# A hybrid decoder layer on one core: the first softmax heads of a set start one group later, and the gated GLA rows are turned one step later

## Chip, core and metric

The kernel runs on one core of a Trainium2 chip, in one launch. The metric is the device time of that launch in microseconds, the median of several executions. TensorE (PE in the profile) multiplies, VectorE (DVE) and ScalarE (ACT) do the elementwise work, GpSimd (POOL) does a few small steps, and SyncE (SP) issues nearly all DMAs, in order.

## The reference, cut to what matters

One layer, 512 tokens, width 2048, float32. After a first RMSNorm one projection feeds two groups of heads: four heads of gated linear attention (GLA), whose rows are normalised and multiplied by silu of a gate, and eight softmax heads. Both results go through `w_out`, and a SwiGLU block of hidden width 5632 follows.

```python
h = rms_norm(x, norm1_g[l])
proj = h @ w_in[l]
qa, ka, va, ra, ga, qb, kb, vb = jnp.split(proj, split_points, axis=-1)
...
out_a = gla_mixer(qa, ka, va, ra, log_g, gla_onorm_g[l])   # ... * silu(ra)
out_b = dilated_mixer(rms_norm(qb), rms_norm(kb), vb, rel_bias)
mix = jnp.concatenate([out_a, out_b], axis=-1)
x = x + mix @ w_out[l]
h2 = rms_norm(x, norm2_g[l])
x = x + (silu(h2 @ w_gate[l]) * (h2 @ w_up[l])) @ w_down[l]
```

(Reshapes are left out here.) For the softmax heads the three dilated branches, merged by their denominators, come to one causal softmax over 512 keys with a bias table per distance.

## The kernel before

**The stream of products.** All large matrix products are done as pairs of 512 columns (`Pair`, L199). A pair's product over 512 rows and 1024 columns is computed by a Strassen-like scheme of seven products P1 to P7 on operand blocks A11, A12, A22 and sums S1 to S4. Each product takes four *groups* of 256 contraction rows, so a pair has 28 groups. `stream` (L301) runs all pairs in one loop over groups. For each group a weight tile of 128x1024 is needed as it is or as a difference of two tiles (`source`, L219; the subtraction is L230 on VectorE); ScalarE casts its high part (`wh`, L320), VectorE makes the low part (`wl`, L324), and TensorE runs eight products with `wh` and then four with `wl` (L364). The buffers for `wh` and `wl` are two each, so the casts run about one group ahead of TensorE. In this document groups are counted in TensorE's order from 1: the first pair is 1 to 28, the four projection pairs after it 29 to 140, the pair of the GLA gate columns 141 to 168 ("gate pair"), and the first pair of `w_out` begins at 169.

**The work between the products.** In the middle of each group, between the `wh` and the `wl` products, the pair's `step` is called (L371). It first counts down what was put off with `later` (L503 to L512) and then takes units from the generators in `background`, in the order of the list, until it has spent as many units as the pair's pace allows (L515 to L523). `soon` (L377) puts something off by whole groups. `ensure` (L328) hurries the background when the next group's operand is not made yet. The order in which the instructions land on an engine follows from this emission and from the scheduler of the framework, and it is fixed when the program is built; each engine and the SP queue then run in that order.

**The softmax heads.** `dil_heads(h)` (L1052) runs two heads in two lanes. Stage 0 of `dil_head` (L962) issues the loads of q, k (L981), v (L985) and the bias table (L987); stage 1 scales q on ScalarE (L991); the stages after it compute scores (L999), add bias and take the maximum on VectorE (L1004), exponentiate on ScalarE (L1008), scale on VectorE (L1014, L1015), turn the result on TensorE (L1026, copied back at L1029) and multiply with the values (L1033, copied at L1036). The last stage stores the head to `mix_d` (L1049). Heads 0 to 3 are set 0 and run in the groups from 113 on; heads 4 to 7 are set 1 and run in the gate pair. After stage 0 of the first heads of a set (h = 0 and h = 4) the generator yields once more than the others (L1062).

**What reads the heads.** `early_jobs` (L1249) loads finished heads back (`top`, L1226), splits them as A11 (L178 on ScalarE, L179 on VectorE), and subtracts their halves (`differ`, L1264 on VectorE) for S3. `late_jobs` (L1285) makes S1, S2, S4, A12 and A22 from heads and gated rows (L1295, L1297, L1299). All are operands of the `w_out` pairs.

**The gated rows.** The gate pair ends in `final_gate` (L1191), once for each of four blocks (half, which): first (0,0), then (1,1), (0,1), and (1,0) out of the accumulators after the last product. It multiplies the normalised GLA rows with the gate column (L1207, or L1200), builds the sigmoid on ScalarE with three activations (L1208 or L1205, L1209, L1210), and two groups later `rest` multiplies both (L1214) and puts `transposed_store` (L1158) off with `later`. That does eight transposes on TensorE (L1165), two copies on ScalarE (L1173) and two stores to `mix_d` (L1180).

Of the kernel before, what the change touches and what calls it, by code (L numbers as in the profile page):

```python
# [108 lines left out]
def block_kernel(ctx: ExitStack, tc: tile.TileContext, ins, out):  # L109
# [19 lines left out]
    def nm(s):  # L129
        uid[0] += 1  # L130
        return f"{s}_{uid[0]}"
# [4 lines left out]
    def bank():  # L136
        return ps.tile([P, 512], F32, name=nm("bank"), tag="bank")

    def work(tag, shape=(P, 512), bufs=1):
        return mp.tile(list(shape), F32, name=nm(tag), tag=tag, bufs=bufs)  # L140
# [51 lines left out]
    def unfolded(t):  # L192

        return t.rearrange("p (a b) -> p b a", b=2)

    def halves(t):
        return t.rearrange("p (b a) -> p b a", b=2)
# [179 lines left out]
    def soon(fn, groups=1):  # L377

        soonest.append([groups, fn])
# [123 lines left out]
    def later(units, fn, hold=False):  # L503

        deferred.append([units, fn, hold])
# [546 lines left out]
    def dil_heads(h):  # L1052

        lanes = [dil_head(h, 0), dil_head(h + 1, 1)]
        for i in range(8):
            for n, lane in enumerate(lanes):
                for rest in next(lane) or ():
                    rest()
                if i == 7 and n == 1:
                    done.update((id(mix_d[4 + h // 2]), half) for half in range(2))  # L1060
                yield 0.5
            if i == 0 and h % 4 == 0:  # L1062
                yield

    def together(*gens):

        gens = list(gens)
        while gens:
            spent = WAIT
            for g in list(gens):  # L1070
                try:
                    cost = next(g)
                except StopIteration:
                    gens.remove(g)
                    cost = 0.0
                cost = 1.0 if cost is None else cost
                if cost >= 0:
                    spent = max(spent, 0.0) + cost
            yield spent
# [23 lines left out]
    def heads_norm(t, then):  # L1103
# [8 lines left out]
        def rest():  # L1112
# [11 lines left out]
        "va0": lambda: [gla_head(0), gla_head(1)],  # L1124
        "va1": lambda: [gla_head(2), gla_head(3)],
        "vb0": lambda: [dil_heads(0), dil_heads(2)],
        "qb1": lambda: [
            together(dil_heads(4), put_off(8, early_jobs(opm, (0, 1), mix_d[4:], True))),
            together(dil_heads(6), put_off(2, early_jobs(opm, (2,), mix_d[4:], True)), late_opm[0]),
            early_jobs(opm, (3,), mix_d[4:], True),  # L1130
            late_opm[1],
# [26 lines left out]
    def transposed_store(tiles, half, dsts, gains=None, spare=None):  # L1158

        for b in range(2):  # L1160
            bk = bank().rearrange("p (j n) -> p j n", j=2)
            for jj in range(2):
                for m in range(2):
                    f = (2 * b + jj) * P
                    nc.tensor.transpose(  # L1165
                        bk[:, jj, m * P : (m + 1) * P], tiles[m][:, f : f + P], ident
                    )
            if spare is None:
                d = work(("oT", "PT")[b], (P, 2, 256))
            else:  # L1170
                d = spare[:, b]
            if gains is None:
                nc.scalar.copy(d, bk)  # L1173
            else:
                for jj in range(2):
                    nc.scalar.activation(
                        d[:, jj, :], bk[:, jj, :], AF.Copy,
                        scale=gains[:, 2 * b + jj : 2 * b + jj + 1],
                    )
            store(dsts[b][:, :, half * 256 : (half + 1) * 256], d)  # L1180
            done.add((id(dsts[b]), half))
# [9 lines left out]
    def final_gate(half, which, tiles, acc_):  # L1191
        og = onorm.pop((half, which))
        if tiles is None:
            tiles = [cpool.tile([P, 512], F32, name=nm("cr"), tag="C") for _ in range(2)]
            src = acc_
        else:
            src = tiles
        for m in range(2):
            if src is acc_:
                nc.vector.scalar_tensor_tensor(  # L1200
                    halves(og[m]), unfolded(src[m]), row_scale(half, m), halves(og[m]),
                    op0=ALU.mult, op1=ALU.mult,
                )
                neg = nrs1[:, 2 * half + m : 2 * half + m + 1]
                nc.scalar.activation(halves(tiles[m]), unfolded(src[m]), AF.Exp, scale=neg)  # L1205
            else:
                nc.vector.tensor_tensor(og[m], src[m], og[m], op=ALU.mult)  # L1207
                nc.scalar.activation(tiles[m], src[m], AF.Exp, scale=-1.0)  # L1208
            nc.scalar.activation(tiles[m], tiles[m], AF.Ln, bias=1.0)  # L1209
            nc.scalar.activation(tiles[m], tiles[m], AF.Exp, scale=-1.0)  # L1210

        def rest():
            for m in range(2):
                nc.vector.tensor_tensor(tiles[m], tiles[m], og[m], op=ALU.mult)  # L1214
            spare = apool.tile([P, 2, 2, 256], F32, name=nm("turned"), tag="A")
            later(1 + (src is tiles), lambda: transposed_store(
                tiles, half, mix_d[2 * which : 2 * which + 2], spare=spare
            ))

        soon(rest, 2)  # L1220
# [561 lines left out]
```

## Time and profile before

| what | value |
|---|---|
| median of three runs | 1939.63 us (1934.64 to 1940.75) |
| the profiled execution's own time | 1940.65 us |
| its span, first to last instruction | 1938.9 us |
| mean granted TensorE clock | 0.997 |
| DMA, mean over the span | 187 GB/s |

The profile shows one execution. A timeline row reads: start, duration, engine, line, operation, output and inputs, how many, and in square brackets the idle time before it and what ended it. A row of the waits reads: who waited at which line for whom; total us, times, longest us. In rows of stretches each engine has its busy time and its number of instructions, and after them stand the granted clock of TensorE, the DMA share and GB/s. Idle time of an engine that is not the bottleneck costs nothing.

### The profile page before, as it was taken

What the parts mean: (1) busy time and instruction counts of PE and PEld (TensorE: products, weight loads), DVE (VectorE), ACT (ScalarE), POOL (GpSimd) and SP (SyncE); (2) the same over time, 40 slices, a digit from 0 to 9 for tenths busy, and PEclk for the clock granted to TensorE, in tenths of its full rate; (3) what the DMA queues carried; (4) which work ended last, traced back from release to release, by engine and by line L of the source; (5) the groups of instructions that cost most, each with busy time, mean ns of one, the idle gap of its engine ahead of it and who ended that gap; (6) DMA issues with size and microseconds to landing.
All of it is one profiled execution on the core that took longest, in us unless ns stands there. A gap on an engine that the chain in (4) does not pass through costs nothing.

```text
span 1938.9 us, 25475 instructions
## 1 busy us (share of the span) xinstructions
PE 1904.8 (98%) x8986; PEld 1645.9 (85%) x8986; DVE 1684.6 (87%) x1915; ACT 1068.7 (55%) x1550; POOL 59.2 (3%) x80
## 2 busy tenths in 40 slices
PE   8999999999999999999999999999999999999999
PEld 7888888887888878888888888888888888888887
DVE  8997887876999889979879879879879989989987
ACT  8564564566775776545545545444446546546443
POOL 1000221011000001000000000000000000000000
PEclk9999999999999999999999999999999999999999
DMA  8358365467675685554554554554555785965761
GB/s 282 132 164 281 102 188 147 143 197 198 180 260 187 215 300 172 168 183 135 170 184 133 166 181 128 166 182 127 167 182 181 226 268 179 282 206 169 252 218 65
DMA packets 341800, 362.01 MB, mean 187 GB/s; under 512 B 132790, under 2 KB 202623, under 8 KB 341672
## 3 DMA queue, kind: packets, MB, share of 16 engines
q1 hardware_dynamic: 341320, 360.17, 59.5%
q8 instruction: 70, 1.15, 0.2%
q14 instruction: 58, 0.48, 0.1%
q10 hardware_dynamic: 352, 0.21, 0.0%
HBM read 298.16 MB, written 64.51 MB: 187 GB/s over the span
## 4 chain that ended last, share of the span: by engine, by line
PE 77%; DVE 12%; DMA 5%; issue 4%; ACT 2%; SPq 0%; POOL 0%; DVEq 0%; ACTq 0%; POOLq 0%
PE acc L364 70%; DVE wl L324 4%; PE acc L432 2%; DVE wa L230 2%; DMA wc<-in_w_gate 1%; PE bank L1033 1%; DVE AS L179 1%; DVE wb L230 1%; PE bank L999 1%; ACT wh L320 1%; DMA top<-mix_d 1%; PE bank L1026 0%; DMA mix_d<-r 0%; PE bank L785 0%; DMA qT<-qb 0%
## 5 line engine op out<-in xcount | busy, mean ns | idle before, releaser
L364 PE MATMUL acc<-wh,AS 128*128 128x512 f32 x3008 | 710.9, 379 | 0.0
L364 PEld LDWEIGHTS acc<-wh,AS 128*128 128x128 f32 x3008 | 568.3, 189 | 81.1 <-issue 0.2
L320 ACT CAST wh<-wa 128x1024 fp32r<-128x1024 f32 x376 | 394.1, 1049 | 391.7 <-PE acc L364 357.7
L364 PE MATMUL acc<-wh,AA 128*128 128x512 f32 x2256 | 536.6, 380 | 5.1 <-ACT wh L320 4.8
L324 DVE TENSOR_TENSOR wl<-wa,wh 128x1024 fp32r<-128x1024 f32 x376 | 457.5, 1218 | 56.8 <-ACT wh L320 51.1
L364 PEld LDWEIGHTS acc<-wh,AA 128*128 128x128 f32 x2256 | 427.2, 190 | 68.7 <-ACT wh L320 7.0
L364 PE MATMUL acc<-wl,AS 128*128 128x512 f32 x1504 | 395.9, 385 | 6.5 <-DVE wl L324 6.2
L364 PEld LDWEIGHTS acc<-wl,AS 128*128 128x128 f32 x1504 | 279.7, 189 | 58.7 <-DVE wl L324 17.9
L364 PE MATMUL acc<-wl,AA 128*128 128x512 f32 x1128 | 296.4, 385 | 2.1 <-DVE wl L324 1.9
L364 PEld LDWEIGHTS acc<-wl,AA 128*128 128x128 f32 x1128 | 211.9, 190 | 37.6 <-DVE wl L324 7.7
L320 ACT CAST wh<-wb 128x1024 fp32r<-128x1024 f32 x94 | 98.6, 1049 | 129.0 <-PE acc L364 113.6
L320 ACT CAST wh<-wc 128x1024 fp32r<-128x1024 f32 x94 | 98.2, 1046 | 108.4 <-PE acc L364 104.2
L230 DVE TENSOR_TENSOR wa<-wc,wa 128x1024 f32<-128x1024 f32 x94 | 114.6, 1223 | 48.4 <-DMA wc<-in_w_gate 29.8
L320 ACT CAST wh<-wd 128x1024 fp32r<-128x1024 f32 x94 | 98.6, 1049 | 102.9 <-PE acc L364 99.9
L324 DVE TENSOR_TENSOR wl<-wc,wh 128x1024 fp32r<-128x1024 f32 x94 | 114.7, 1221 | 38.8 <-ACT wh L320 37.3
L324 DVE TENSOR_TENSOR wl<-wd,wh 128x1024 fp32r<-128x1024 f32 x94 | 114.5, 1222 | 19.4 <-ACT wh L320 13.7
L324 DVE TENSOR_TENSOR wl<-wb,wh 128x1024 fp32r<-128x1024 f32 x94 | 113.8, 1218 | 5.4 <-ACT wh L320 5.4
L230 DVE TENSOR_TENSOR wb<-wd,wb 128x1024 f32<-128x1024 f32 x94 | 114.8, 1221 | 0.6
L230 DVE TENSOR_TENSOR wa<-wb,wa 128x1024 f32<-128x1024 f32 x94 | 113.7, 1220 | 1.6 <-DMA wb<-in_w_down 0.9
L230 DVE TENSOR_TENSOR wa<-wd,wa 128x1024 f32<-128x1024 f32 x94 | 113.0, 1220 | 0.0
L281 DVE SCALAR_TENSOR_TENSOR seed<-acc,rs,seed 128x512 f32<-128x512 f32 x96 | 70.4, 747 | 22.1 <-PE acc L364 22.1
L265 ACT ACTIVATE seed<-acc,rs 128x512 f32<-128x512 f32 x96 | 60.6, 681 | 0.8 <-PE acc L364 0.8
(309 smaller groups left out, 1319.1 us busy)
## 6 DMA issues: line engine op xcount, KB each, us to landing
wa<-in_w_gate SPq DMA_DIRECT2D x44, 512.0 KB, 4.3
wb<-in_w_up SPq DMA_DIRECT2D x44, 512.0 KB, 4.4
wd<-in_w_up SPq DMA_DIRECT2D x44, 512.0 KB, 3.9
wc<-in_w_gate SPq DMA_DIRECT2D x44, 512.0 KB, 3.5
wc<-in_w_in SPq DMA_DIRECT2D x32, 512.0 KB, 4.1
wa<-in_w_in SPq DMA_DIRECT2D x24, 512.0 KB, 5.4
wb<-in_w_in SPq DMA_DIRECT2D x24, 512.0 KB, 5.8
wd<-in_w_in SPq DMA_DIRECT2D x24, 512.0 KB, 6.7
```

The costliest lines, as they stand in the source:

```text
L179: nc.vector.tensor_tensor(low, src, high.bitcast(F32), op=ALU.subtract)
L230: nc.vector.tensor_tensor(src, minuend, src, op=ALU.subtract)
L265: nc.scalar.activation(halves(t), unfolded(src[m]), AF.Copy, scale=self.scale(half, m))
L281: nc.vector.scalar_tensor_tensor(halves(seed[m]), unfolded(src[m]), self.scale(half, m), halves(seed[m]), op0=ALU.mult, op1=ALU.add,)
L320: nc.scalar.copy(high[k], sources[k])
L324: nc.vector.tensor_tensor(low[k], sources.pop(k), high[k].bitcast(F32), op=ALU.subtract)
L364: nc.tensor.matmul(p.dst[prod][m], a[:, jj, hl, m * P : (m + 1) * P], folded(w[:, jj, :]), start=fresh and g == 0 and len(terms) == 2 and ...
L432: recent["pe"] = nc.tensor.matmul(dst[prod][m], a[:, jj, hl, m * P : (m + 1) * P], folded(w[:, jj, :]), start=fresh and g == 0 and len(ter ...
L999: nc.tensor.matmul(lp[:, :n], qh[:, b * P : (b + 1) * P], kh[:, :n], start=True, stop=True)
L1033: nc.tensor.matmul(op, vh[:, k, :], lgs[b][:, k * P : (k + 1) * P], start=(k == 0), stop=(k == b))
```

## The change

```diff
@@ dil_heads
             if i == 0 and h % 4 == 0:
                 yield
+                yield
 
     def together(*gens):
@@ final_gate, rest
             spare = apool.tile([P, 2, 2, 256], F32, name=nm("turned"), tag="A")
-            later(1 + (src is tiles), lambda: transposed_store(
+            later(3 - (src is acc_), lambda: transposed_store(
                 tiles, half, mix_d[2 * which : 2 * which + 2], spare=spare
             ))
```

The first edit makes the generator of heads 0 and 1, and that of heads 4 and 5, give back one more unit after their loads. The units of everything behind it in the list come later by as much. The second raises the count of `later` from 2 to 3 for the three blocks that come as tiles, and from 1 to 2 for the block that comes out of the accumulators (`src is acc_`). No instruction is added or taken away; the order changes on TensorE in groups 113 to 171.

## Prediction

> **What bounds the kernel now.** I read the page's totals first, then TensorE's waits by stretch, then the streams of the engines around the two longest waits.
>
> ```profile
> span 1938.9 us, 25475 instructions
> ...
> PE 1904.8 (98%) x8986; PEld 1645.9 (85%) x8986; DVE 1684.6 (87%) x1915; ACT 1068.7 (55%) x1550; POOL 59.2 (3%) x80
> ```
>
> TensorE (PE) sets the time: 34 us of the span are without a product. Only what lengthens or removes its waits counts, and the speed at which its clock lets it run. Its waits where the change works, 460 to 580 us, and before that, 340 to 460 us:
>
> ```profile
> PE bank L1026 <- DVE L L1015: 4.2, 2, 3.4
> PE bank L1165 <- DVE seed L1214: 2.1, 1, 2.1
> PE acc L364 <- ACT wh L320: 0.8, 1, 0.8
> ...
> PE acc L364 <- ACT wh L320: 0.9, 1, 0.9
> PE acc L364 <- DVE wl L324: 0.5, 1, 0.5
> ```
>
> The last two lines are set 0 of the softmax heads: 1.4 us in 120, and neither is a head's product. The first three are the gate pair, with heads 4 to 7 and the gated rows. In order of time:
>
> ```profile
> 467.65 1.89 PE L364 MATMUL acc<-wh,AA 128*128 128x512 f32 x8
> ...
> 471.16 2.00 PE L364 MATMUL acc<-wh,AA 128*128 128x512 f32 x8 [0.76 <-ACT wh L320]
> ...
> 479.99 0.48 PE L1026 MATMUL bank<-mats,L 128*128 128x128 f32 x1 [3.36 <-DVE L L1015]
> ...
> 521.82 0.44 PE L1026 MATMUL bank<-mats,L 128*128 128x128 f32 x2 [0.86 <-DVE L L1015]
> ...
> 560.82 1.04 PE L1165 MATMUL bank<-mats,seed 128*128 128x128 f32 x7 [2.14 <-DVE seed L1214]
> ```
>
> In the count of the section on the kernel the first two rows are groups 147 and 148, the third lies in 149, the last in 169. Half-microsecond stretches show the granted clock (third number from the end) after the two long waits:
>
> ```profile
> 479.50:480.00 0.50, 0.01 (x1) 0.01 (x2) 0.50 (x3) 0.00 (x0) 0.00 (x0) 0.70 1.03 401
> 483.00:483.50 0.50, 0.50 (x3) 0.19 (x1) 0.50 (x1) 0.50 (x3) 0.00 (x0) 0.89 0.00 0
> ...
> 561.50:562.00 0.50, 0.50 (x4) 0.50 (x3) 0.50 (x2) 0.50 (x3) 0.00 (x0) 0.62 1.07 391
> 565.00:565.50 0.50, 0.50 (x4) 0.39 (x3) 0.50 (x2) 0.50 (x2) 0.00 (x0) 0.97 0.89 315
> ```
>
> Between each two of these rows the clock is 0.50: about 3.4 us at half speed each time, so 1.7 us of work lost each time. Why L1015 was late is in ScalarE's, VectorE's and the queue's streams:
>
> ```profile
> 461.72 0.37 SPq L981 DMA_DIRECT2D q<-qb  x1
> 462.15 3.83 SPq L1049 DMA_DIRECT2D mix_d<-r  x1
> 466.02 0.44 SPq L981 DMA_DIRECT2D qT<-qb  x1
> ...
> 468.85 2.57 SPq L1226 DMA_DIRECT2D top<-mix_d  x4
> ...
> 467.26 0.72 ACT L991 ACTIVATE q<-q,gq 128x512 f32<-128x512 f32 x1 [1.82 <-DMA q<-qb]
> 469.46 0.72 ACT L991 ACTIVATE qT<-qT,gq 128x512 f32<-128x512 f32 x1 [1.47 <-DMA qT<-qb]
> 470.08 1.98 ACT L320 CAST wh<-wa 128x1024 fp32r<-128x1024 f32 x2
> ...
> 473.95 0.69 DVE L1264 TENSOR_TENSOR top<-top 128x512 f32<-128x512 f32 x1 [0.44 <-DMA top<-mix_d]
> 476.58 0.69 DVE L1264 TENSOR_TENSOR top<-top 128x512 f32<-128x512 f32 x1 [1.94 <-DMA top<-mix_d]
> 477.19 0.28 DVE L1004 CUSTOM_DVE_ANT_0 L<-bank,T 128x128 f32<-128x128 f32 x1
> ...
> 477.61 0.75 DVE L281 SCALAR_TENSOR_TENSOR seed<-acc,rs,seed 128x512 f32<-128x512 f32 x1
> 478.28 0.32 DVE L1014 RECIPROCAL mx<-mx 128x1 f32<-128x1 f32 x2
> 478.51 1.22 DVE L324 TENSOR_TENSOR wl<-wa,wh 128x1024 fp32r<-128x1024 f32 x1
> 479.65 0.28 DVE L1015 TENSOR_SCALAR L<-L,mx 128x128 f32<-128x128 f32 x1
> ```
>
> ScalarE stood at L991 for loads, two casts were late, VectorE then stood at both L1264 for loads, and the first head's L1004 and L1015 were queued behind. The 2.14 us have the same cause: a third L1264 in front of the second L1214.
>
> ```profile
> 558.34 0.69 DVE L1264 TENSOR_TENSOR top<-top 128x512 f32<-128x512 f32 x1 [1.84 <-DMA top<-mix_d]
> ...
> 560.08 0.68 DVE L1214 TENSOR_TENSOR seed<-seed,og 128x512 f32<-128x512 f32 x1
> ```
>
> **Set 0, first edit.** In the streams as built, the scores L999 of heads 0 and 1 go from groups 113 and 115 to 115 and 117, and the last values from 144 to 146. L991 of these heads stays. Nothing waited there, so nothing can be saved. I cost it at zero; what hides it is VectorE's free time, 13.7 of 60 us:
>
> ```profile
> 400.00:460.00 60.00, 59.54 (x305) 51.62 (x304) 46.33 (x76) 39.63 (x118) 11.54 (x16) 1.00 0.67 195
> ```
>
> If that cover failed, the tightest place is group 143, where the last L1015 of head 2 now stands behind an L1114 that waits for POOL: 1 us.
>
> **Set 1, first edit.** The scores move from group 148 (both heads) to 149 and 150, and no L1026 stays in 149. Gone: 0.76 and 3.36, one half-clock stretch (1.7), and 0.86 in 160, whose L1015 no longer comes late in my walk. But L991 of head 4 goes the other way: it now stands in front of the cast for group 147, not behind it, and the queue now has kT, q, qT in one row ahead of mix_d5, so qT no longer waits 3.83 us behind that store. q still has to wait for the stores of qb and lands at about 467.3 as now. Then L991 (0.72) and the cast (1.05) end at 469.0, up to 469.5 if q shares the DMA engines with kT; group 147 could start at 467.65. Wait: 1.4 to 1.9, I take 1.6. (If q landed before 465.9 it would be 0.) Groups 148 and 149 follow 2.6 us apart.
>
> The first top load is now queued behind mix_d5<-oT, which needs ScalarE after that cast: issue near 470.3 and 470.9. Its landing takes 4.2 us in the median, 5.1 at 468.85:
>
> ```profile
> top<-mix_d SPq DMA_DIRECT2D x8, 256.0 KB, 4.2
> ```
>
> So 475.1 to 475.5. VectorE's order behind it is L1264, wl, L281, wl, L281, L1004, L1207, wl, L1014, L1207, L1015. By the rows above, from start to start: 0.61 (L1264), 1.14 (each wl), 0.67 (each L281), 0.21 (L1004), and 0.6 for each L1207, a 128x512 product like L1264: 7.1 us. The first wl is then ready at 477.0, 0.7 late for group 149. L1015 ends at 482.3, where TensorE arrives at about 480.2 with half of group 150 done: 2.0. The wait has thus not vanished; it is 2.6 us of products further on and shorter. For both I keep the ends 0.5 (top lands 2 us sooner) and 4.5 (q later by 2).
>
> The second L1264 now comes in group 151 behind eleven other instructions and finds its data. Groups 152 to 166: 0.2 in all.
>
> **Second edit.** Each later() count rises by one, so every transposed_store (8 transposes, 2 casts, 2 stores) goes one group down: 152 to 153, 167 to 168; the third, (0,1), stays in 169 and the last, (1,0), in 171 and 172, where the built order has them before and after. The stores of mix_d0 and mix_d1 have their readers moved too, from 157 to 159; nothing waits. The transposes in 169 now use rows that VectorE finishes in 168, in front of L1264, which has moved to 170 with heads 6 and 7: 2.14 and its half-clock stretch (1.7) go. What is late next is what stands behind L1264 in 170: wl, two L230 and L1214 for (1,0), about 4.1 us with L1264 itself. The last store and its load run
>
> ```profile
> 548.29 0.34 SPq L1049 DMA_DIRECT2D mix_d<-r  x1
> ...
> 553.64 1.19 SPq L1226 DMA_DIRECT2D top<-mix_d  x2
> ...
> 572.80:600.00 27.20, 25.97 (x118) 21.87 (x118) 26.67 (x31) 18.83 (x28) 0.00 (x0) 1.00 0.35 114
> ```
>
> 10 us from store to data now (548.29 to 558.34), and the store would leave near 547 to 548: data at 557 to 558, just when VectorE gets there. Then L1214 ends near 562.5 and group 171 stands for it from about 561: 1.5 (0 to 3). After 572.8 VectorE is busy 26.67 of 27.20 us, so a lead gained before is kept, not widened.
>
> **Sum.** Gone: 0.76 + 3.36 + 0.86 + 2.14 + 1.7 + 1.7 = 10.5. New: 1.6 + 0.7 + 2.0 + 0.2 + 1.5 = 6.0. Net -4.5. The profiled execution took 1940.65 us (1.75 outside its span), so 1936.2; it is 1.0 above the median 1939.63 of the runs, for which I forecast 1935.1, as 1935. New waits between 2.2 (1.0 + 0.5 + 0.2 + 0.5) and 12 (1.9 + 4.5 + 0.2 + 3 + 2.4 for q later by as much as one more group), and none to two half-clock stretches (0 to 3.4), give -8 to +5 before any mishap in set 0.
>
> The clock decides part of it. Here 0.86 us of waiting kept the full clock, 2.14 and 3.36 lost it; the two falls lie about 82 us apart, 24 times 3.4. The Trainium skill, "TensorE: Matmul & The Clock Gate", Part 1 and "HAM oscillation", says that the clock is judged in free-running windows of about 3.4 us and asks for no idle gaps above about 3.4 us. The windows agree with this trace; the limit does not, since 2.14 us were enough. By that limit neither old wait would have cost clock, and the sum would be 7.1 less 6.0, -1.1.
>
> **Rivals.** (1) The waits move whole: VectorE's backlog puts L1015 in 150 as far back as it was in 149 and the new wait of 2.0 becomes 3.4 with half clock again, the one in 171 becomes 2.5. New: 6.0 + 1.4 + 1.7 + 1.0 = 10.1, so 1939. For it: VectorE is the engine behind both old waits and its work is unchanged. Against: one L230 and one L1264 leave the crowded stretch. That the edit does not do what it says (L991 stands earlier, not later) ends here too.
>
> (2) Clean: the loads land early enough, new waits are 2, net -8.5: 1931. For it: qT's 3.83 us behind a store are gone. Against: ScalarE meets q one cast earlier.
>
> (3) Slower: kT, q and qT, three loads of runs of 128 bytes, go out together; q lands late and holds ScalarE in front of the cast for 147, which nothing covers. Each us beyond 467.3 is one us of TensorE, and beyond 2 us also 1.7 of clock. Break-even is a landing near 470; at 475 the term is 9.1 + 1.7 in place of 1.6, net +4.7, and with half clock again at 150 +6.4: 1946. For it: the landing of q alone took 5.5 us (461.72 to 467.26). Against: q had other loads and a store beside it then as well. The Trainium skill, "DMA: Bandwidth & Descriptors", "Why small descriptors are slow (HBM only)", tells of a fixed overhead for each such run, which would be on this rival's side; no run here shows the three together.
>
> **How the numbers follow.** Forecast 0.46, centred on 1935, from 1932 to 1938; (1) 0.12; (2) 0.22; (3) 0.20. About 0.3% (5.8 us) is what a measurement of this kernel can tell from no change, since its own three runs span 6.1 us. Below 1933.8 lie all of (2) and two fifths of the forecast: 0.41. Above 1945.4: (3), and a mishap in set 0 with 0.01: 0.21. Between: 0.38. The likeliest case's own range is 1932 to 1938; for 8 in 10 it has to reach into (2) and (3): 1930 to 1946.
>
> **What would show it.** Right: no wait in 149 at L1026 and none at L1165 in 169; a wait of 1 to 2 us on the cast for 147 after L991; a wait of about 2 us at the first L1026 in 150, on L1015; about 1.5 us in 171; from 572.8 on the old stream, some 5 us earlier. Wrong: q landing beyond 470; half clock behind 150 or 171; a wait in set 0; a wait of L230 or L320 for weights, which would say that the load queue was reordered against the kernel.

## Result, and the profile after

| | before | after |
|---|---|---|
| median | 1937.87 us (1934.64 to 1940.75, 5 runs) | 1929.17 us (1928.62 to 1931.36, 5 runs) |
| the profiled execution's own time | 1940.65 us | 1928.62 us |
| its span | 1938.9 us | 1926.8 us |

The change makes the kernel faster: 8.7 us between the medians, ratio 0.9961 with a 95% interval of 0.995 to 0.9972. The two profiled executions lie further apart, 12.0 us, since that of before was 2.8 us above its median. Lines behind L1063 have moved down by one: L1265 after is L1264 before, L1215 is L1214, L1166 is L1165.

The totals of the page after:

```profile
span 1926.8 us, 25472 instructions
...
PE 1900.7 (99%) x8986; PEld 1642.7 (85%) x8986; DVE 1684.6 (87%) x1915; ACT 1070.6 (56%) x1550; POOL 58.0 (3%) x80
```

TensorE is without a product for 26 us in place of 34, and busy for 4.1 us less with the same number of products; 4.0 of these lie in the stretch shown further down, most of them the clock. TensorE's waits from 460 to 580 us, after:

```profile
PE bank L1166 <- DVE cr L1215: 1.2, 1, 1.2
PE acc L364 <- DVE wl L324: 0.6, 1, 0.6
PE bank L1026 <- DVE r L1015: 0.2, 1, 0.2
```

4.2, 2.1 and 0.8 us of before have become 1.2 in group 171, 0.2 in group 162, and 0.6 at 579.7 us, which lies behind the stretch of the next rows. The stretch from the start of group 147 to the start of group 173, as rows of stretches, before and then after:

```profile
467.65:572.84 105.19, 97.95 (x497) 83.02 (x496) 91.63 (x153) 73.09 (x145) 0.00 (x0) 0.97 0.74 226
```

```profile
465.95:561.39 95.44, 93.96 (x497) 80.16 (x496) 88.56 (x151) 72.22 (x142) 0.00 (x0) 1.00 0.77 241
```

9.75 us fewer for the same 497 products, at a granted clock of 1.00 in place of 0.97: the waits in it fall from 7.1 to 1.4 us, and two half-clock stretches, 3.4 us of work, are gone. The rest of the 12.1 us between the spans is 1.70 us ahead of group 147 and 0.65 us behind group 173. The 1.70 are not the change's doing: this execution was ahead by 1.5 us at group 113 already (355.39 against 356.92), where the order begins to differ.

The cause is in the queue. This row of before tells when it issues the last stores of qb1, which the loads of q have to wait for:

```profile
454.01 5.66 SPq L1098 DMA_DIRECT2D qb<-cout  x8
```

And the queue's, ScalarE's, VectorE's and TensorE's rows of after:

```profile
448.94 5.55 SPq L1099 DMA_DIRECT2D qb<-cout  x8
...
456.24 1.07 SPq L981 DMA_DIRECT2D q<-qb  x1
457.37 1.25 SPq L981 DMA_DIRECT2D qT<-qb  x1
...
463.03 1.63 SPq L1227 DMA_DIRECT2D top<-mix_d  x2
...
460.12 0.72 ACT L991 ACTIVATE q<-q,gq 128x512 f32<-128x512 f32 x1
...
462.06 0.72 ACT L991 ACTIVATE qT<-qT,gq 128x512 f32<-128x512 f32 x1
...
469.30 0.69 DVE L1265 TENSOR_TENSOR top<-top 128x512 f32<-128x512 f32 x1 [1.87 <-DMA top<-mix_d]
...
473.58 0.28 DVE L1004 CUSTOM_DVE_ANT_0 L<-bank,T 128x128 f32<-128x128 f32 x1
...
476.18 0.28 DVE L1015 TENSOR_SCALAR L<-L,mx 128x128 f32<-128x128 f32 x1
...
479.69 0.67 DVE L1265 TENSOR_TENSOR top<-top 128x512 f32<-128x512 f32 x1
...
476.52 0.33 PE L1026 MATMUL bank<-mats,L 128*128 128x128 f32 x1
...
557.23 0.41 PE L1166 MATMUL bank<-mats,cr 128*128 128x128 f32 x2 [1.17 <-DVE cr L1215]
```

The stores go out 5.1 us earlier, q 5.5 us earlier (456.24 against 461.72), qT 8.7, the first top loads 5.8; of each of these the execution's lead at group 113 is 1.5. ScalarE runs both L991 without idle time; before it waited 1.82 and 1.47 there. VectorE still waits 1.87 for the first top load, but at 469.3, and no product waits for that. L1015 ends at 476.46 and TensorE begins the first L1026 at 476.52: no wait, with hardly 0.1 us to spare.

### The profile page after: what moved, and what is told of

Read it like the earlier page. It is cut to its first block, busy times and chain, and to the rows that moved or that the text cites. A ratio compares the mean times of both kernels' runs of the same rounds, so it can differ in the third digit from the quotient of the medians.

```text
span 1926.8 us, 25472 instructions
## 1 busy us (share of the span) xinstructions
PE 1900.7 (99%) x8986; PEld 1642.7 (85%) x8986; DVE 1684.6 (87%) x1915; ACT 1070.6 (56%) x1550; POOL 58.0 (3%) x80
## 4 chain that ended last, share of the span: by engine, by line
PE 68%; DVE 11%; issue 3%; DMA 3%; ACT 1%; POOL 0%; DVEq 0%; SPq 0%; ACTq 0%; POOLq 0%
PE acc L364 66%; DVE wl L324 5%; DVE wa L230 2%; DVE AS L179 1%; PE bank L1033 1%; PE bank L999 1%; DVE wb L230 1%; ACT wh L320 0%; DVE AA L179 0%; DMA wc<-in_w_gate 0%; PE bank L1026 0%; DVE seed L281 0%; DMA top<-xn_d 0%; DMA r<-xn_d 0%; DMA x_d<-seed 0%
## 5 line engine op out<-in xcount | busy, mean ns | idle before, releaser
L320 ACT CAST wh<-wc 128x1024 fp32r<-128x1024 f32 x94 | 98.4, 1047 | 113.1 <-PE acc L364 108.7
L320 ACT CAST wh<-wd 128x1024 fp32r<-128x1024 f32 x94 | 98.5, 1048 | 99.1 <-PE acc L364 96.9
```

The costliest lines, as they stand in the source:

```text
L320: nc.scalar.copy(high[k], sources[k])
```

## Experiments

In the texts written ahead of the runs, theory A says that the gain comes from when set 0 runs: its delayed products let the stores of qb1 leave early, so q and the top loads come early and L1264 is out of the way. Theory B says that each edit removes the wait it is aimed at; theory C, from the second batch on, that the place of L1264 alone decides.

Each kernel was timed against the kernel before on the same chip, in five rounds. The first four ran on one chip (before: median 1942.61 us), the next four on a second (1943.3), the last three on a third (1942.47). "147 to 173" is the time from the first product of group 147 to that of group 173 in the run's trace.

| kernel | ratio, 95% interval | 147 to 173, us |
|---|---|---|
| before | 1 | 105.2 |
| the change, first measurement | 0.9961 (0.995 to 0.9972) | 95.4 |
| first edit alone | 0.9957 (0.9945 to 0.997) | 96.3 |
| second edit alone | 0.9986 (0.9977 to 0.9994) | 101.4 |
| unit for set 0 alone | 0.9961 (0.9949 to 0.9973) | 95.9 |
| unit for set 1 alone | 1.0 (0.9989 to 1.0011) | 104.4 |
| before, both L1264 away (14 units) | 0.9967 (0.9956 to 0.9978) | 99.9 |
| before, one L1264 away (12 units) | 1.001 (1.0 to 1.0019) | 107.8 |
| unit for set 0, one L1264 away (10 units) | 0.9979 (0.9969 to 0.9989) | 98.5 |
| the change again | 0.9954 (0.9939 to 0.997) | 95.4 |
| unit for set 0, and second edit | 0.9984 (0.9974 to 0.9994) | 100.1 |
| the change with two units for one | 0.9991 (0.9982 to 1.0001) | 98.4 |
| the change, both L1265 away (14 units) | 0.9992 (0.9981 to 1.0003) | 98.7 |

### Which edit brings it

First edit alone:

```diff
             if i == 0 and h % 4 == 0:
                 yield
+                yield
```

> The first edit alone (one more unit for both sets; the gated rows stay as before). Theory A, the gain comes from when set 0 runs (its units put off let the stores of qb1 go out about 5 us earlier, so q is there when ScalarE asks for it, and L1264 no longer stands in front of the first head): nearly the whole gain, ratio to before 0.996 to 0.997; no wait at L1026 in group 149 or 150, and none over 1 us at the transposes in 168 either, since the third L1264 has moved to 170 with the heads. Theory B, each edit removes its own wait: about half, ratio 0.9975 to 0.9985, with the 2.1 us wait at the transposes still there.

Second edit alone:

```diff
-            later(1 + (src is tiles), lambda: transposed_store(
+            later(3 - (src is acc_), lambda: transposed_store(
```

> The second edit alone (gated rows one step later, heads as before). Theory A: the wait at L1026 behind L1015 stays (3.4 us with half clock, or moved to group 150 at 2 to 3 us), the 2.1 us at the transposes shrink to under 1; ratio 0.998 to 1.000. Theory B: half of the gain, ratio 0.9975 to 0.9985, with the wait at L1026 unchanged.

The unit for one set only, in the first run for set 0, in the second for set 1:

```diff
                 yield
+                if h == 0:
+                    yield
```

> One more unit for heads 0 and 1 only, gated rows as before. Theory A: q of head 4 lands before ScalarE reaches L991 (about 5 us earlier in its load than before), the tops are split over groups 148 and 151, no wait over 1 us from 460 to 520; ratio 0.996 to 0.998. Rival, the unit of set 1 gives the loads their time: ratio 0.999 to 1.001, with the wait at L1026 of 2 to 3.4 us still there.

```diff
                 yield
+                if h == 4:
+                    yield
```

> One more unit for heads 4 and 5 only, gated rows as before. Theory A: q is issued as late as before (about 461.7), ScalarE waits 1.5 to 2 us for each of q and qT, both L1264 still stand in front of the first L1004, and the wait at L1026 only moves to group 150 with 1.5 to 3 us; ratio 0.998 to 1.000. Rival: no wait over 1 us there, ratio 0.996 to 0.997.

The first edit alone does as much as the change (0.9957), and of it the unit for set 0 alone (0.9961); the unit for set 1 alone does nothing (1.0). The second edit alone gains a little, 0.14%. In the run with the first edit alone 0.76 us of waiting at L1026 stay in group 150, where theory A had expected none. Rows of the run with set 0's unit:

```profile
449.83 5.55 SPq L1100 DMA_DIRECT2D qb<-cout  x8
...
457.13 1.08 SPq L981 DMA_DIRECT2D q<-qb  x1
...
463.07 0.32 SPq L1049 DMA_DIRECT2D mix_d<-oT  x1
...
463.92 1.91 SPq L1228 DMA_DIRECT2D top<-mix_d  x2
...
461.01 0.72 ACT L991 ACTIVATE q<-q,gq 128x512 f32<-128x512 f32 x1
...
442.94 1.89 PE L364 MATMUL acc<-wh,AA 128*128 128x512 f32 x8
```

And of the run with set 1's unit, on the same chip:

```profile
453.17 5.67 SPq L1100 DMA_DIRECT2D qb<-cout  x8
...
460.88 0.37 SPq L981 DMA_DIRECT2D q<-qb  x1
461.30 3.81 SPq L1049 DMA_DIRECT2D mix_d<-r  x1
...
467.97 2.57 SPq L1228 DMA_DIRECT2D top<-mix_d  x4
...
466.39 0.72 ACT L991 ACTIVATE q<-q,gq 128x512 f32<-128x512 f32 x1 [1.79 <-DMA q<-qb]
...
445.63 1.89 PE L364 MATMUL acc<-wh,AA 128*128 128x512 f32 x8
...
470.24 2.00 PE L364 MATMUL acc<-wh,AA 128*128 128x512 f32 x8 [0.68 <-ACT wh L320]
...
475.55 0.69 DVE L1266 TENSOR_TENSOR top<-top 128x512 f32<-128x512 f32 x1 [1.56 <-DMA top<-mix_d]
...
478.61 0.28 DVE L1004 CUSTOM_DVE_ANT_0 L<-bank,T 128x128 f32<-128x128 f32 x1
...
481.16 0.48 PE L1026 MATMUL bank<-mats,L 128*128 128x128 f32 x1 [2.59 <-DVE L L1015]
```

With set 0's unit TensorE comes to group 141 2.7 us earlier than with set 1's (442.94 against 445.63) and to group 147 at the same time (466.83 and 466.80): the products of heads 0 to 3 that left the groups up to 143 are done in 144 to 146. What does not wait for them, the end of the last projection pair and its stores, leaves earlier by 3.3 us. In the queue q and qT then stand ahead of both stores of heads 2 and 3, and top goes out 4.1 us earlier. With set 1's unit nothing of this moves. The scores are then indeed a group later and the wait in 149 is gone, but 2.59 us of it stand in 150. That is close to the 2.0 us which the prediction expected there of the whole change. Two half-clock stretches follow it, 3.4 us of work.

In the run with the second edit alone, only half of what is saved is where that edit was made. The other half is here:

```profile
473.78 0.68 DVE L1264 TENSOR_TENSOR top<-top 128x512 f32<-128x512 f32 x1
474.38 0.28 DVE L1004 CUSTOM_DVE_ANT_0 L<-bank,T 128x128 f32<-128x128 f32 x1
...
477.71 0.33 PE L1026 MATMUL bank<-mats,L 128*128 128x128 f32 x1 [1.49 <-DVE L L1015]
```

The reordering took the second L1264 from 149 to 151, out of the way of L1004, which comes at 474.38 in place of 477.19. The wait at L1026 falls from 3.36 to 1.49 us and keeps the full clock, 3.6 us in all, which neither theory had expected. The 2.14 us at L1165, which that edit aims at, are gone in this run with their half clock (3.8 us), and also in the runs with the first edit or the unit of either set alone. Other waits of 0.4 to 1.1 us come up, and in all the stretch is 3.8 us shorter.

### Early q, or L1264 out of the way

The jobs that issue the top loads and L1264 are put off by 8 units in the kernel before. Put off by more, L1264 moves while q stays late:

```diff
-            together(dil_heads(4), put_off(8, early_jobs(opm, (0, 1), mix_d[4:], True))),
+            together(dil_heads(4), put_off(14, early_jobs(opm, (0, 1), mix_d[4:], True))),
```

> The kernel before, with the early jobs of the first pair of set 1's heads put off by 14 units in place of 8: both first L1264 now stand in group 154, well behind the first heads' L1004, and nothing of set 0 is moved, so q still lands near 467. Theory A (set 0's earlier end lets q land early, and this is what the change brings): q stays late, so L991 waits as before (about 1.8 and 1.5 us) and a cast wait of about 0.8 us in group 148 stays, as does 2.1 us at L1165 with its half clock, but L1004 no longer stands behind L1264, so the 3.36 us in 149 shrink to under 1 us and keep the full clock. Gone: at most 3.4 + 1.7 = 5 us; ratio 0.9975 (0.997 to 0.9985). Theory C (the place of L1264 alone makes the gain, q does not matter): as much as the change itself, ratio about 0.996. If q's lateness alone holds up the first heads, the wait in 149 stays over 2 us and the ratio is 0.999 to 1.

The same line with 12 in place of 14:

> The kernel before, with the same jobs put off by 12 units: one L1264 stays in group 149, in front of the first L1004, the other moves to 151; q is late as before. Theory A: the L1264 that stays found its data within 0.44 us, the one that moves waited 1.94 and ran 0.61, so L1004 comes about 2.5 us earlier and the 3.36 us in 149 fall to about 1 us at full clock; L991's waits and the cast's 0.76 stay; the third L1264 stands in 168. Ratio 0.998 (0.997 to 0.999), if the load still lands at 474. Theory C: with one L1264 still in front of L1004 most of the loss stays: ratio 0.999 to 1.

And set 0's unit with 10, where the L1264 stand in the same two groups as with 12:

> One unit more for set 0 alone (as in the run with h == 0), and the same jobs put off by 10, so that the L1264 stand in 149 and 151 as in the run before this one, but q comes early. Theory A: no wait at L991, cast in time, no wait over 1 us at L1026 in 149 or 150; ratio 0.996, and 0.001 to 0.002 less than the kernel with L1264 in the same groups and q late: what the early q is worth by itself. Theory C: the same ratio as that kernel, since the L1264 stand alike.

The change itself on the chip of these runs:

> The change itself on the chip of these runs, for comparison. Ratio 0.996 (0.995 to 0.997), no wait over 1.5 us between 460 and 580 us. Theory A: not different from the kernel with one unit more for set 0 alone (0.9961), within 0.001.

It came out at 0.9954, not to be told from set 0's unit alone.

With both L1264 away and q late:

```profile
473.98 0.29 DVE L1004 CUSTOM_DVE_ANT_0 L<-bank,T 128x128 f32<-128x128 f32 x1
...
471.72 1.99 PE L364 MATMUL acc<-wh,AA 128*128 128x512 f32 x8 [1.34 <-ACT wh L320]
```

No product waits for L1015 any more, and 5.3 us of the stretch are gone (105.2 to 99.9); late q costs 1.34 us at a cast. By its ratio, 0.9967, this one number recovers most of the gain without touching a head. It came out better than the 0.9975 of theory A, though its interval takes that in: the 2.1 us at L1165 were gone here too (0.27), which had not been expected.

With one L1264 left in front and q late, nothing is gained:

```profile
468.04 0.43 SPq L185 DMA_DIRECT2D wd<-in_w_in  x1
468.52 2.57 SPq L1226 DMA_DIRECT2D top<-mix_d  x4
...
475.85 0.69 DVE L1264 TENSOR_TENSOR top<-top 128x512 f32<-128x512 f32 x1 [3.42 <-DMA top<-mix_d]
...
479.25 0.47 PE L1026 MATMUL bank<-mats,L 128*128 128x128 f32 x1 [3.70 <-DVE L L1015]
```

Theory A, which forecast 0.998, had assumed that the load lands at 474 as before; theory C's 0.999 to 1 is nearer. The load landed near 475.8: a weight load of 512 KB now went out ahead of it, where before all weight loads of this row stood behind it. So here one waiting L1264 cost as much as two had. With q early and the L1264 in the same groups:

```profile
473.12 0.69 DVE L1266 TENSOR_TENSOR top<-top 128x512 f32<-128x512 f32 x1 [1.67 <-DMA top<-mix_d]
...
478.74 0.33 PE L1026 MATMUL bank<-mats,L 128*128 128x128 f32 x1 [1.20 <-DVE L L1015]
```

The ratio is 0.0031 lower, 6 us, and the stretch 9.3 us shorter (107.8 against 98.5). A weight load goes out ahead of the top loads here too (464.30 against 465.53), so that is not the difference. Theory A had expected more of this kernel, 0.996 and no wait above 1 us. Theory C, by which the place of L1264 alone counts, expected no difference between the two; it falls. Both matter: what holds up TensorE is an L1264 that stands in VectorE's row in front of the first L1004 and whose load has not landed. Moving it away helps, and letting its load go out early helps; the change does both, since one L1265 is done before the scores come and the other comes long after.

### What the other parts do

```diff
                 yield
+                if h == 0:
+                    yield
...
-            later(1 + (src is tiles), lambda: transposed_store(
+            later(3 - (src is acc_), lambda: transposed_store(
```

> One unit more for set 0 alone, together with the second edit: the change without its unit for set 1. Theory A (set 0's unit brings the gain, the other parts little): the same as the change, ratio 0.995 to 0.9965, no wait at L991, the first L1264 in group 148, waits in 460 to 580 us under 2.5 in all. If set 1's unit is needed beside the second edit: ratio 0.997 or more, with a wait of L1026 on L1015 of over 1 us in 149 or 150.

```diff
             if i == 0 and h % 4 == 0:
                 yield
+                yield
+                yield
```

(with the second edit as in the change)

> The change with one unit more for both sets (two beyond the kernel before). Theory A: the gain comes from which instruction stands in front of which, not from the delay itself, so a second unit adds nothing: q early (L991 before 464), but the first L1264 and the heads' products all lie one to three groups later; ratio 0.995 to 0.9975. If the delay itself were what pays: another 2 to 4 us, ratio 0.993 to 0.9945.

The change, with `put_off(14, ...)` for `put_off(8, ...)`:

> The change, with the early jobs of the first pair of set 1 put off by 14 units, so that both first L1264 stand in 155. The change has no wait of L1026 over 0.2 us left, so by theory A nothing is left to gain there: ratio 0.9945 to 0.9965, equal to the change within 0.001. If L1264 still held up VectorE in the change (its first one waited 1.2 to 1.9 us for its load), there would be another 1 to 2 us: ratio 0.994 to 0.9945.

A second unit more does not add to the gain but takes most of it away (0.9991): the delay itself pays nothing, as theory A had it, though the loss is larger than it expected. The other two expectations were missed. Set 0's unit with the second edit keeps less than half of the gain (0.9984), and moving L1265 away in the change costs nearly all of it (0.9992). Waits of TensorE from 460 to 580 us, first of the run with set 0's unit and the second edit, then of the change with L1265 moved:

```profile
PE acc L364 <- ACT wh L320: 2.5, 4, 0.7
PE acc L364 <- DVE wl L324: 0.7, 1, 0.7
PE bank L1026 <- DVE L L1015: 0.6, 2, 0.5
```

```profile
PE acc L364 <- ACT wh L320: 1.3, 2, 0.7
PE bank L1166 <- DVE cr L1215: 1.2, 1, 1.2
PE acc L364 <- DVE wl L324: 1.1, 3, 0.6
PE bank L1026 <- DVE L L1015: 0.6, 1, 0.6
```

In neither is a wait above 1.2 us, and q comes early; but there are nine and seven waits (the smallest left out here), most of them of half a microsecond on casts behind 509 us, where the second pair of heads, L1264 and the gated rows are interleaved anew. The stretch is 4.7 and 3.2 us longer than in the change; the waits in it account for 3.2 and 2.0 of that, and the rest is in no wait of the trace. By the ratios the first run is 4 to 6 us behind the change, which the stretch covers, and the last run 6 to 7, so 3 to 4 lie elsewhere. Behind 580 us it waits 11.3 us on `wl` where the change waited 7.0 and 7.5, but the run with set 0's unit alone waited 11.8 there and kept the gain; this part stays open. These three kernels ran on a chip on which the change itself was not timed; the lengths of the stretch, equal to 0.01 us in the change's two traces, hardly hang on that.

So set 1's unit, worth nothing by itself, is needed beside the second edit: with set 0's unit and the second edit the ratio is 0.9984, with set 1's unit besides it was 0.9961 and 0.9954 on other chips, and the intervals do not overlap. No run shows why the one order suits TensorE and the other does not. The main part of the gain has a shown cause, and its full size belongs to a few interleavings. No other kernel tried was measurably faster than the change.

## Why the prediction was right, and where not

**Sign and size.** The forecast was 1935 (-4.5), the measurement 1929.17 (-8.7). The size that came true is that of the second rival, "Clean": new waits 2, net -8.5, 1931. Its reason holds by half. The loads do land early enough, and qT no longer waits behind a store; but q itself is issued 5.5 us earlier, and no case of the prediction had that. So the rival's number is in part luck. The forecast had what goes right, and what comes in its place too high: 6.0 against a measured 1.4. The range ended at 1930, 0.8 us above the measured time; as a change, -8.7 lies inside it (1930 less 1939.63 is -9.6), since before came out 1.8 us lower over five runs than over three.

**The step that failed** is in the part on set 1: "q still has to wait for the stores of qb and lands at about 467.3 as now." q does wait for these stores, but they leave 5.1 us earlier (3.5 without this execution's lead), and L991 ran at 460.12. The reason stands in the part on set 0, "Nothing waited there, so nothing can be saved. I cost it at zero": the products moved out of groups 113 to 143 were counted as a delay that might cost, and not as time that TensorE gains there for the projection pair whose stores q waits for. The run with set 0's unit alone has the whole gain, and the run with set 1's unit alone, to which the prediction gave most of it, has none.

**What followed from that step.** The 1.6 us at the cast for 147, the 0.7 us for `wl` in 149 and the 2.0 us at L1026 in 150 were all zero. The walk along VectorE was right in itself: 7.1 us from the start of the first L1264 to the end of L1015, measured 7.16 (469.30 to 476.46); only its start, 3.4 us behind that of group 147, came over 4 us earlier than the forecast 475.1 to 475.5, which is 7.5 to 7.9 behind it. With set 1's unit alone, where q is late, such waits came: 0.68 at the cast for 148, and 0.23 for `wl` and 2.59 at L1026 in 150.

**What was right.** 3.36, 0.76, 0.86 (in group 159 of the trace, not 160) and 2.14 are gone, and with the two long ones their two half-clock stretches; the second L1264 found its data (479.69, no wait); groups 152 to 166 cost 0.18 us against 0.2, and group 171 waited 1.17 for `cr` against 1.5. From 173 on the stream is the old one: 1365.4 us to the end of the span (1926.8 less 561.39) against 1366.1 (1938.9 less 572.84). The sum thus is 10.5 less 1.4, 9.1, to which the stretch's 9.75 come close.

**The second edit** was credited with 2.14 and 1.7. The wait does go in its run, but it goes without the edit too, since the first edit already moves L1264 out of 169. Beside the first edit it changes no time that was measured (0.9957 without, 0.9954 and 0.9961 with it); the stretch is 0.8 us shorter with it, the 0.76 us at L1026. Beside set 0's unit alone it does harm (0.9961 without, 0.9984 with it).

**The third rival** priced a late q rightly as what could spoil it, though q came early: its 256 KB landed within 3.7 us beside kT and qT, against 5.5 before.

## What to carry to other kernels

When work is moved out of a stretch where nothing waits, ask what reaches its end earlier there, above all which store some later load depends on, and follow that load through its queue. An instruction that waits for a load in an engine's fixed order costs all that is queued behind it; either move it or let its load go out earlier, and try both one at a time. When an order is interleaved anew, several waits of half a microsecond can return more than the long one that was removed, so a gain from one order need not survive a further step in the same direction.

## What the runs showed of the hardware

**The clock falls in steps.** Granted clock in half-microsecond stretches of the run with one L1264 moved, around its wait of 3.70 us, the first row wholly at half clock, the last of the low stretch and the one behind:

```profile
478.50:479.00 0.50, 0.00 (x0) 0.00 (x0) 0.50 (x2) 0.00 (x0) 0.00 (x0) 0.50 1.06 414
...
485.00:485.50 0.50, 0.50 (x4) 0.41 (x3) 0.50 (x2) 0.00 (x0) 0.00 (x0) 0.80 0.00 0
485.50:486.00 0.50, 0.50 (x4) 0.45 (x3) 0.50 (x4) 0.00 (x0) 0.00 (x0) 1.00 0.00 0
```

One wait here cost two steps, about 6.8 us at half clock. The full-clock time lost around a wait was 0, 1.71 or 3.42 us in all thirteen traces, the first 25 and last 12 us of each span left out. None of the 31 waits from 1.0 to 1.6 us cost any, and all five of 2.9 us or more did. Between 1.8 and 2.9 us 12 of 30 did. It differs at about the same length, as around the wait in the third group of the first SwiGLU pair in the second measurement of the change, and then in the change with L1265 moved:

```profile
717.98 3.92 PE L364 MATMUL acc<-wh,AA 128*128 128x512 f32 x8 [3.17 <-ACT wh L320]
```

```profile
723.38 2.34 PE L364 MATMUL acc<-wh,AA 128*128 128x512 f32 x8 [2.87 <-ACT wh L320]
```

The eight products took 3.92 us at half clock after 3.17 us of waiting, and 2.34 at full clock after 2.87. In the first trace of the change 1.84 us were enough to lose 1.71, in others 2.15 and 2.50 lost nothing.

It depends on where the wait falls. The falls of one trace lie whole multiples of 3.413 us apart: those of before, at 479.70, 561.62 and 728.87, are 24 and 49 of them apart. Cut by this beat, every piece at full clock in which TensorE was without a product for 1.96 us or more was followed by a low one (14 of them), and none with less than 1.70; between, three were and six were not. The 1.84 us above lay in one piece, while the beat cut the 2.87 us into 1.65 and 1.22.

**Only ratios of one measurement compare.** Before, the kernel took 1937.87 us in the first measurement and 1942.5 to 1943.3 on the three chips of the experiments, the change 1929.17 in the first and 1934.66 on one of the three. These 5 us are over half of what the change brings, while its ratio was the same within its interval.
